# Second feed-forward product: 8 of 22 row tiles in seven-product form, and modulation matmuls offered later

## The chip, the cores and the metric

The kernel runs on one core of a Trainium2 chip. The metric is the device time of one execution in microseconds. Five engines run side by side and wait for one another through semaphores: TensorE (PE: matmul, with its weight loads shown apart as PEld), VectorE (DVE), ScalarE (ACT), GpSimd (POOL), and SyncE (SP), which here issues all DMAs, in one order. Matmul results land in PSUM, which has eight banks of 512 fp32 columns in this kernel's use.

## The reference

Two layers of a hybrid decoder. One prompt of 512 positions and 8 sampled sequences of one position each go through the same weights, so a tile of activations has 520 columns. Cut to what matters here:

```python
mod = jax.nn.silu(c) @ ada_w + ada_b          # 1024 -> 6 x 1024 for each of 9 conditions
sh_m, sc_m, gt_m, sh_f, sc_f, gt_f = split(mod, 6)
h = rmsnorm(x, g_pre_mix) * (1 + sc_m) + sh_m
proj = h @ w_in                               # 1024 -> 2816, then retention, two convolutions
mix = concat([o_ret, o_a, o_c]) @ w_out       # 1024 -> 1024
x = x + gt_m * rmsnorm(mix, g_post_mix)
h = rmsnorm(x, g_pre_ffn) * (1 + sc_f) + sh_f
f = (jax.nn.silu(h @ ffn_w1) * (h @ ffn_w3)) @ ffn_w2   # 1024 -> 2816 -> 1024
x = x + gt_f * rmsnorm(f, g_post_ffn)
```

All is fp32.

## The kernel before

**Layout.** Activations stand feature by position: a feature tile is 128 partitions x 520 columns, worked on in two halves of 260 (h = 0 and 1; half 1 holds the sampled columns). An fp32 product is made from parts: each operand is split into a high part (a cast to fp32r, by ACT) and a low part (operand minus high, by DVE or POOL), and `mm3` (L721) issues three matmuls, high x high, high x low and low x high, into one PSUM bank. Weights come in units of 128 x 1024 (512 KB), eight 128 x 128 blocks: a DMA fills one of 3 "raw" buffers, ACT casts it ("wh"), DVE subtracts ("wl"). The split units live in a ring of 8 "w" slots, two to a unit; `ensure_unit` (L682), `ensure_raw` (L654) and `unit` (L1403) claim them in the order of a list of specs. Larger temporaries live in a ring of 22 "s" slots, two big ones ("hh") hold H, the normalized input, and Y, the output.

**Order.** The order of every engine's instructions is fixed when the program is built, by a planner: `Clock` holds estimated times, `Eng` estimates the cost of each operation, background jobs are generators that yield the time at which they want to go on (`at`, L128: the estimated time at which a tile is ready, moved by `lead`), and `mm` moves the planner's time on. `either` (L267) gives an operation to DVE or POOL, whichever the planner expects to end first. On the chip each engine then takes its instructions in that order and waits on semaphores where the estimate was off.

**Modulation.** `ada` (L356) computes a third of the modulation: four times it starts four DMAs of 512 KB of `ada_w`, yields until they are estimated to have landed (L367), and then offers a burst of 16 matmuls (`fill`), which is placed where the planner sees PE waiting, or at the latest a gap after the yield's start (4.5 us in layer 0's input projection, 9 in layer 1's, 12 in layer 0's first feed-forward product). The next four DMAs follow the burst. Two groups of four bursts run beside the input projection of each layer (L1739); `ck.join(ada_bg)` (L1743) has the planner wait for them ahead of the output projection. One more group, for layer 1, runs beside the first feed-forward product.

**First feed-forward product.** 22 row tiles of 128 of the hidden width. Tiles 0 and 1 are plain. Tiles 2 to 21 use a seven-product form (Strassen, Winograd's variant): the 2 x 2 blocks are w1 and w3 by two halves of the depth, against the two halves of the depth by two halves of the columns. `zprep` (L743) makes seven split weight products ("wz", each 128 x 512, one w slot) named A11, S1, S2, A12, S3, A22 and S4; `Operands` makes the sums T1 to T4 of H; `zproduct` (L838) does 4 x 3 matmuls for a product. Sums of products are formed in PSUM, by going on in a bank or a copy of it. The gated result stays in `FT` (pairs of row tiles, fp32) and `fparts` splits it into `F` (high, low).

**Second feed-forward product** (L2009 to L2040). For each output tile m of 8 and half h, 22 row tiles are summed in one bank: 66 matmuls. Tile 0 does both halves side by side, in the order in which `F` becomes ready. A weight unit serves both halves; in layer 0 half 1 of tile 5 comes last, with its three units read again; the first two units of tile 6 stand in an hh buffer ("wq"). ACT copies each bank to Y and squares it for the norm. When half 0 has its eight tiles, a `Chain` (L569) applies the norm and the gate, adds to x and, in layer 0, makes H for layer 1's input projection, while PE does what is left of half 1.

## Time and profile before

| | |
|---|---|
| time, median of 3 runs | 1208.46 us (1208.44 to 1209.1) |
| the profiled execution's own time | 1211.95 us |
| its span, first to last instruction | 1210.1 us |
| mean granted TensorE clock | 0.993 |
| bytes moved by DMA | 175.52 MB, 145 GB/s on average |
| second product of layer 0 | 489.13 to 616.62 us |
| second product of layer 1 | 1071.86 to 1198.60 us |

The page gives busy times of engines, the chain of work that ended last, and groups of instructions by cost. Nearly all DVE, ACT and POOL instructions have the line of one helper (L176) and nearly all matmuls that of `mm` (L243), so groups are told apart by tile names: "ps<-s,wz" is a matmul into PSUM with a wz weight and an operand in an s slot, "s,sc" a modulation matmul, "t,one" the matmul that sums squares over partitions. In the stretches view each engine's busy time is followed by its count of instructions; the three figures at the end are the granted clock, the DMA engines' share and GB/s. In the order of time a row has start, duration, engine, and in brackets the idle time before it and what ended it; PE's instructions overlap, so starts are compared, not durations.

### The profile page before, as it was taken

How to read it: one execution, taken by the hardware profiler on the slowest of the kernel's cores; microseconds unless marked ns; L12 is line 12 of the kernel's file. 1: busy time of each engine (PE TensorE's matmuls, PEld its weight loads, DVE VectorE, ACT ScalarE, POOL GpSimd, SP SyncE). 2: the span in 40 equal slices, each digit the busy share in tenths (PEclk: the TensorE clock that was granted, in tenths of full speed). 3: DMA queues.
4: the chain of work that ended last, by engine and by line, in shares of the span. 5: the costliest groups of instructions: out<-in, count | busy, mean ns of one | idle time of the engine just before them, and what ended most of it. 6: DMA issues, size and time to landing. Idle time of an engine off the chain costs nothing.

```text
span 1210.1 us, 24224 instructions
## 1 busy us (share of the span) xinstructions
PE 1187.4 (98%) x9795; PEld 1124.7 (93%) x9795; DVE 885.5 (73%) x1608; ACT 624.8 (52%) x1254; POOL 155.6 (13%) x155
## 2 busy tenths in 40 slices
PE   9999999999999999999999999999999999999996
PEld 8878779999989999999988879899999999999996
DVE  6679868689979988623493489878999998882234
ACT  6553454577546556623352354466765555582221
POOL 0284102011100000000004334200110000010001
PEclk9999999999999999999999999899999999999998
DMA  8578674424673232333365854343323343142222
GB/s 310 223 193 254 237 261 83 145 87 143 214 254 123 89 124 81 114 96 101 113 250 215 266 169 144 71 141 104 123 73 109 135 140 114 61 127 81 83 77 72
DMA packets 71073, 175.52 MB, mean 145 GB/s; under 512 B 23857, under 2 KB 28593, under 8 KB 70961
## 3 DMA queue, kind: packets, MB, share of 16 engines
q1 hardware_dynamic: 70960, 173.97, 44.0%
q8 instruction: 77, 1.26, 0.4%
q14 instruction: 36, 0.29, 0.1%
HBM read 166.74 MB, written 5.08 MB: 142 GB/s over the span
## 4 chain that ended last, share of the span: by engine, by line
PE 80%; DVE 9%; ACT 3%; DMA 3%; POOL 2%; issue 2%; SPq 1%; POOLq 0%; DVEq 0%; ACTq 0%
PE ps L243 80%; DVE s L176 3%; DVE t L176 2%; DMA s<-in_ada_w_dram 2%; POOL s L176 2%; DVE wl L176 1%; DVE ps L176 1%; DVE H L176 1%; ACT s L176 1%; SPq L258 1%; PE ps L253 1%; ACT wh L176 1%; ACT t L176 1%; ACT L176 1%; ACT H L176 0%
## 5 line engine op out<-in xcount | busy, mean ns | idle before, releaser
L243 PE MATMUL ps<-s,wh 128*128 128x260 f32 x1536 | 277.5, 283 | 0.0
L243 PE MATMUL ps<-s,wz 128*128 128x260 f32 x1920 | 246.3, 283 | 0.3 <-ACT ps L176 0.2
L243 PEld LDWEIGHTS ps<-s,wz 128*128 128x128 f32 x1920 | 236.6, 188 | 3.7 <-issue 2.5
L243 PEld LDWEIGHTS ps<-s,wh 128*128 128x128 f32 x1536 | 236.9, 188 | 0.3
L243 PE MATMUL ps<-H,wh 128*128 128x260 f32 x1184 | 228.7, 292 | 1.4 <-ACT s L176 1.0
L243 PE MATMUL ps<-s,wl 128*128 128x260 f32 x768 | 216.8, 282 | 0.0
L243 PEld LDWEIGHTS ps<-H,wh 128*128 128x128 f32 x1184 | 185.5, 191 | 20.0 <-issue 15.1
L176 DVE TENSOR_TENSOR wl<-raw,wh 128x1024 fp32r<-128x1024 f32 (+1 forms) x92 | 115.3, 1259 | 78.3 <-ACT wh L176 77.8
L243 PE MATMUL ps<-H,wl 128*128 128x260 f32 x592 | 168.4, 284 | 0.3 <-DVE wl L176 0.3
L243 PE MATMUL ps<-H,wz 128*128 128x260 f32 x1104 | 147.8, 283 | 0.0
L243 PEld LDWEIGHTS ps<-s,wl 128*128 128x128 f32 x768 | 144.5, 188 | 0.0
L243 PEld LDWEIGHTS ps<-H,wz 128*128 128x128 f32 x1104 | 138.5, 188 | 1.2 <-issue 0.8
L176 ACT CAST wh<-raw 128x1024 fp32r<-128x1024 f32 (+1 forms) x95 | 94.9, 1009 | 38.3 <-PE ps L243 27.8
L176 ACT CAST wz<-raw 128x512 fp32r<-128x512 f32 x144 | 87.7, 620 | 51.3 <-DVE raw L176 39.8
L243 PEld LDWEIGHTS ps<-H,wl 128*128 128x128 f32 x592 | 113.0, 191 | 0.6 <-DVE wl L176 0.6
L176 DVE TENSOR_TENSOR wz<-raw,wz 128x512 fp32r<-128x512 f32 x144 | 97.8, 687 | 16.9 <-ACT wz L176 14.9
L243 PE MATMUL ps<-H,s 128*128 128x260 f32 (+1 forms) x816 | 106.1, 285 | 1.3 <-ACT s L176 1.3
L243 PEld LDWEIGHTS ps<-H,s 128*128 128x128 f32 x816 | 100.9, 188 | 4.4 <-issue 2.1
L176 DVE TENSOR_TENSOR t<-t,t 128x260 f32<-128x260 f32 x99 | 42.1, 431 | 80.0 <-ACT t L176 78.1
L176 DVE TENSOR_TENSOR wz<-s,wz 128x512 fp32r<-128x512 f32 x108 | 73.7, 686 | 16.6 <-ACT wz L176 15.9
L176 ACT COPY s<-ps 128x260 f32<-128x260 f32 (+1 forms) x83 | 35.4, 434 | 92.1 <-PE ps L243 70.0
L243 PE MATMUL ps<-s,s 128*128 128x260 f32 (+3 forms) x672 | 79.3, 287 | 0.0
(166 smaller groups left out, 1585.0 us busy)
## 6 DMA issues: line engine op xcount, KB each, us to landing
raw<-in_w_dram SPq DMA_DIRECT2D x102, 512.0 KB, 3.6
s<-in_ada_w_dram SPq DMA_DIRECT2D x80, 512.0 KB, 6.3
raw<-in_w_in_dram SPq DMA_DIRECT2D x38, 512.0 KB, 4.5
s<-in_w_dram SPq DMA_DIRECT2D x34, 512.0 KB, 5.2
raw<-in_w_dram SPq DMA_DIRECT2D x25, 384.0 KB, 4.2
s<-in_ada_dram SPq DMA_DIRECT2D x16, 512.0 KB, 7.5
raw<-in_w_out_dram SPq DMA_DIRECT2D x16, 512.0 KB, 4.6
X<-in_xT_dram SPq DMA_DIRECT2D x4, 520.0 KB, 5.5
```

Of the source, the lines that this page charges most:

```text
L176: f(*args, **kw)
L243: PE.matmul(out, lhsT, rhs, start=start, stop=stop, skip_group_check=True)
L253: PE.transpose(out, in_, ident[:n, :n])
L258: nc.sync.dma_start(out=out, in_=in_)
```

## The change

**Second feed-forward product.** Its 22 row tiles are taken in three pieces, with the running sum kept in Y between them. First row tiles 16 to 21, plain, for all eight output tiles (tiles 0 and 1 side by side, row tiles 16 to 19 ahead of 20 and 21); the banks are copied to Y. Then row tiles 8 to 15 in the seven-product form: the 2 x 2 blocks are two output tiles by two groups of four row tiles, against the two groups by the two halves of the columns, four pairs of output tiles. A job `names` makes the split operands B11, B22, B21 and T1 to T4 from `FT[3]` to `FT[6]`, in part in an hh buffer (`ext`); `zprep` makes the weight products with the w2 blocks (tag "zz") as its raw data; `plus` adds the results into Y. Last row tiles 0 to 7, plain, first half 0 of all output tiles, then half 1 (tile 7 first): `back` has ACT copy Y into a bank two jobs ahead, the matmuls go on summing there, and the result is copied to Y as before. The weights of this piece are read once for each half, except for tile 7; the rereading of tile 5 in layer 0 and the buffer "wq" go.

**Split of the gated rows.** `fparts` takes a list of pairs: pairs 7 and 8 (row tiles 16 to 19) at the end of the first product, pairs 0 to 2 (2 to 7) during the seven products. Pairs 3 to 6 are no longer split themselves.

**Modulation.** The job yields until 3 us after the estimated landing of its weights in place of the landing itself; with a gap that is over by then, the burst is placed at once. This holds for all five groups.

**Weight supply.** `ensure_unit` returns where no slot or raw buffer is free, and `unit` lets the planner's time go on until there is one.

```diff
--- before.py
+++ after.py
@@ -364,7 +364,7 @@
                 dma(r, ada_w[l, k1 * 128:(k1 + 1) * 128, c0:c0 + 1024], ck.now)
                 ts.append(r)
             t0 = ck.now
-            yield at(*ts)
+            yield ck.at(*ts, lead=-3.0)
             if ps is None:
                 ps = bank()
...
             if rawlive["raw"] == 3:
-                if tag != "z" or rawlive["s"] >= 2:
+                if tag[0] != "z" or rawlive["s"] >= (2 if tag == "z" or zspare[0] else 1):
                     return
...
-    def zprep(l, t):
+    def zprep(l, t, pairs=()):
...
+        for p in pairs:
+            order += [(p, "A11"), (p, "S1")] + [(p - 1, "A22"), (p - 1, "S4")] * (p > pairs[0])
+            order += [(p, "S2"), (p, "A12"), (p, "S3")]
+        if pairs:
+            order += [(pairs[-1], "A22"), (pairs[-1], "S4")]
...
+                if pairs:
+                    j1, j3 = U["w2", l, 2 * (i - pairs[0]), 1], U["w2", l, 2 * (i - pairs[0]) + 1, 1]
...
-        for j in ([U["w1", l, NZ], U["w3", l, NZ]] if NZ < NF else [U["w2", l, 0, 0], U["w2", l, 0, 1]]):
+        for j in [U["w2", l, 0, 0], U["w2", l, 1, 0]] if pairs else [U["w2", l, 0, 2], U["w2", l, 1, 2]]:
...
         for m in range(KT):
-            for u in range(3):
-                n = min(8, NF - 8 * u)
-                U["w2", l, m, u] = spec(w2[l, m, :, u * 1024:u * 1024 + n * 128], n=n,
-                                        tag=f"q{u}" if m == 6 and u < 2 else "w")
-        if l < DEPTH - 1:
-            for u in range(3):
-                n = min(8, NF - 8 * u)
-                U["w2", l, KT, u] = spec(w2[l, MR, :, u * 1024:u * 1024 + n * 128], n=n)
+            U["w2", l, m, 2] = spec(w2[l, m, :, 2048:2048 + 768], n=6)
+        for m in range(KT):
+            U["w2", l, m, 1] = spec(w2[l, m, :, 1024:2048], tag="zz")
+        for m in range(KT):
+            U["w2", l, m, 0] = spec(w2[l, m, :, 0:1024])
+        for m in range(KT - HOLD):
+            U["w2", l, m, 3] = spec(w2[l, m, :, 0:1024])
 
...
     def unit(key, ahead=2):
         i = U[key]
         ensure_unit(i)
+        while i not in units:
+            ck.wait()
+            ensure_unit(i)
...
-        def fparts():
-            n = len(FT)
-            for j in range(n):
-                while j >= allow[0]:
+
+        def fparts(js):
+            for n, j in enumerate(js):
+                while n >= allow[0]:
                     yield 0.05
-                src = FT[j] if j < n - 1 else fx[0]
+                src = FT[j]
                 p = slot(F32R), slot(F32R)
...
-                ck.start(fparts())
+                allow[0] = ALLOW[0]
+                ck.start(fparts([7, 8]))
...
-        jobs = [(m, h) for m in range(6) for h in range(2)] + [(6, 0), (7, 0), (7, 1), (6, 1)]
-        if not last:
-            jobs.remove((MR, 1))
...
+        def names():
+
+            def src(q, h):
+                return [FT[3 + 2 * q + n][:, :, cols(h)] for n in range(2)]
+
+            def put(name, x, home=None):
+                for n in range(2):
+                    t = slot(F32R, (128, 2, 2, HW)) if home is None else ext[:, home + 2 * n:home + 2 * n + 2]
+                    yield at(x[n])
+                    S.copy(out=t[:, :, 0, :], in_=x[n])
+                    yield at(t[:, :, 0, :])
+                    yield from turn(-1)
+                    V.tensor_tensor(out=t[:, :, 1, :], in0=x[n], in1=t[:, :, 0, :], op=sub)
+                    nt.setdefault(name, []).append(t)
+
+            def tsum(x, y, z):
+                for n in range(2):
+                    yield from turn(-1)
+                    V.tensor_tensor(out=x[n], in0=y[n], in1=z[n], op=sub)
+
+            b11, b12, b21, b22 = src(0, 0), src(0, 1), src(1, 0), src(1, 1)
+            yield from put("B11", b11)
+            yield from tsum(b11, b12, b11)
+            yield from put("T1", b11, 0)
+            yield from put("B22", b22)
+            yield from tsum(b12, b22, b12)
+            yield from tsum(b22, b22, b11)
+            yield from put("T2", b22, 4)
+            yield from put("B21", b21)
+            yield from tsum(b21, b21, b22)
+            while not zspare[0]:
+                yield 0.05
+            yield from put("T3", b12)
+            yield from put("T4", b21)
+
+        zspare[0] = False
+        ck.start(names(), 6.0)
+        P0 = NF + 1
+        ck.start(zprep(l, ck.now, list(range(P0, P0 + 4))))
...
+        acc = [(m, h, bank()) for m in range(2) for h in range(2)]
+        for ks in (range(16, 20), range(20, NF)):
+            for m in range(2):
+                un = unit(("w2", l, m, 2), 1)
+                for k in ks:
+                    while k not in F:
+                        ck.wait()
+                    for m1, h, ps in acc:
+                        if m1 == m:
+                            whole2(m, 2, h, k, un, ps, k == 16, k == NF - 1)
+        for m, h, ps in acc:
+            S.copy(out=Y[:, h, m, :], in_=ps[:, :HW])
+        for m in range(2):
+            free_unit(("w2", l, m, 2))
+        for m in range(2, KT):
+            un = unit(("w2", l, m, 2), W2A)
+            for h in range(2):
+                ps = bank()
+                for k in range(16, NF):
+                    whole2(m, 2, h, k, un, ps, k == 16, k == NF - 1)
+                S.copy(out=Y[:, h, m, :], in_=ps[:, :HW])
+            free_unit(("w2", l, m, 2))
+        for k in range(16, NF):
+            del F[k]
+        zspare[0] = True
+        allow[0] = 3
+        mp, ybg = {}, {}
+        def zq(p, b, ps, name, first, copied=None):
+            while len(nt.get(name, ())) < 2:
+                ck.wait()
+            zproduct(l, P0 + p, b, ps,
+                     lambda k: (nt[name][k // 2][:, k % 2, 0, :], nt[name][k // 2][:, k % 2, 1, :]), first, copied)
+        def plus(h, m, x):
+            def job():
+                yield atp(x) if in_psum(x) else at(x)
+                either(Y[:, h, m, :], x, Y[:, h, m, :], add)
+            ybg.setdefault((h, m), []).append(ck.start(job()))
+        def m_first(p):
+            a, d = bank(), bank()
+            zq(p, "A11", a, "B11", True)
+            b = bank()
+            S.copy(out=b[:, :HW], in_=a[:, :HW])
+            zq(p, "S1", d, "T1", True)
+            mp[p] = [a, d, b]
+        def m_up(p):
+            a, x3 = mp[p][0], mp[p][3]
+            zq(p, "A22", a, "T4", False, x3)
+            plus(0, 2 * p + 1, a[:, :HW])
+        def m_gate(p):
+            d = mp.pop(p)[1]
+            zq(p, "S4", d, "B22", False)
+            plus(1, 2 * p, d[:, :HW])
+        for p in range(4):
+            m_first(p)
+            if p == 0:
+                ck.start(fparts([0, 1, 2]))
+            else:
+                m_up(p - 1)
+                m_gate(p - 1)
+            a, d, b = mp[p]
+            zq(p, "S2", a, "T2", False)
+            x2 = tmp()
+            S.copy(out=x2, in_=a[:, :HW])
+            plus(1, 2 * p, x2)
+            zq(p, "A12", b, "B21", False, b[:, :HW])
+            plus(0, 2 * p, b[:, :HW])
+            zq(p, "S3", a, "T3", False, x2)
+            x3 = tmp()
+            S.copy(out=x3, in_=a[:, :HW])
+            plus(1, 2 * p + 1, d[:, :HW])
+            plus(1, 2 * p + 1, x3)
+            mp[p].append(x3)
+        jobs = [(m, 0) for m in range(KT)]
+        jobs += [(m, 1) for m in range(KT - HOLD, KT)] + [(m, 1) for m in range(KT - HOLD)]
...
+        def back(n):
+            m, h = jobs[n]
+            for x in ybg[h, m]:
+                ck.join(x)
+            ps = bank()
+            S.copy(out=ps[:, :HW], in_=Y[:, h, m, :])
+            pre.append(ps)
+        back(0)
+        back(1)
+        for n, (m, h) in enumerate(jobs):
+            ps = pre[n]
+            if n == 1:
+                m_up(3)
+            if n == KT:
+                m_gate(3)
+            if n + 2 < len(jobs):
+                back(n + 2)
+            key = ("w2", l, m, 3 if h and m < KT - HOLD else 0)
+            while key not in units and U[key] not in units and wlive[0] > 6:
+                ck.wait()
+            un = unit(key, W2A)
+            ck.to(max(ck.now, ck.ready(ps[:, :HW])))
+            for k in range(8):
...
+                whole2(m, 0, h, k, un, ps, False, k == 7)
+            if h == 1 or m < KT - HOLD:
+                free_unit(key)
+            if not last and h == 1:
+                ensure_unit(U["in", l + 1, KGRP], U[key])
```

## The prediction

> **What bounds the kernel now.** I read the page from the top: span, busy time, chain that ended last.

> ```profile
> span 1210.1 us, 24224 instructions
> ...
> PE 1187.4 (98%) x9795; PEld 1124.7 (93%) x9795; DVE 885.5 (73%) x1608; ACT 624.8 (52%) x1254; POOL 155.6 (13%) x155
> ...
> PE 80%; DVE 9%; ACT 3%; DMA 3%; POOL 2%; issue 2%; SPq 1%; POOLq 0%; DVEq 0%; ACTq 0%
> ```

> TensorE (PE) is busy 98% and is 80% of the chain: fewer matmuls is time, provided that what feeds them keeps up. Whether it does is read by stage, in the stretches view (PE, weight load, DVE, ACT, sometimes POOL, then clock, DMA share, GB/s).

> ```profile
> 361.00:421.00 60.00, 60.00 (x503) 59.18 (x495) 52.44 (x98) 35.78 (x78) 0.00 (x0) 1.00 0.34 114
> ...
> 489.13:616.62 127.49, 127.49 (x1063) 127.30 (x1062) 56.11 (x87) 50.52 (x86) 1.63 (x2) 1.00 0.33 102
> ...
> 593.00:617.00 24.00, 24.00 (x199) 23.81 (x198) 20.47 (x42) 13.66 (x25) 1.63 (x2) 1.00 0.32 106
> 617.00:640.00 23.00, 22.05 (x175) 19.67 (x174) 21.68 (x43) 13.12 (x28) 4.42 (x5) 1.00 0.87 328
> ```

> The first row lies in the first feed-forward product, which already has the seven-product form: DVE is busy 52.44 of 60 us (87%) and PE still never idles. The second is the whole second product of layer 0 (489.13 is its first matmul, 616.62 the first of layer 1): there DVE has 71 us free. The last two are the passage into layer 1, where DVE is busy 20.47 of 24 and 21.68 of 23: nearly the bound, and PE begins to lose time.

> The other losses of PE are waits. The order of time shows the modulation matmuls ("s,sc") that wait for their weights, and what one burst of 16 costs undisturbed (640.90 to 642.76):

> ```profile
> 82.26 1.65 PE L243 MATMUL ps<-s,sc 128*32 128x512 f32 x8
> 85.08 1.05 PE L243 MATMUL ps<-s,sc 128*32 128x512 f32 x4 [1.17 <-DMA s<-in_ada_w_dram]
> 87.45 1.75 PE L243 MATMUL ps<-s,sc 128*32 128x512 f32 x4 [1.32 <-DMA s<-in_ada_w_dram]
> 89.12 0.80 PE L243 MATMUL ps<-H,wh 128*128 128x260 f32 x2
> ...
> 91.18 0.40 PE L243 MATMUL ps<-H,wh 128*128 128x260 f32 x2
> ```
> ```profile
> 640.90 1.92 PE L243 MATMUL ps<-s,sc 128*32 128x512 f32 x16
> 642.76 0.51 PE L243 MATMUL ps<-H,s 128*128 128x260 f32 x2
> ```
> ```profile
> 677.14 1.96 PE L243 MATMUL ps<-s,sc 128*32 128x512 f32 x12
> 679.77 1.05 PE L243 MATMUL ps<-s,sc 128*32 128x512 f32 x4 [0.67 <-DMA s<-in_ada_w_dram]
> 680.75 0.50 PE L243 MATMUL ps<-H,wh 128*128 128x260 f32 x2
> ```

> **Part one: the seven-product form.** Before, each layer does 8 output tiles x 22 row tiles x 2 halves x 3 matmuls = 1056. After: 6 row tiles plain (288), 8 row tiles as 4 pairs x 7 products x 4 x 3 = 336 in place of 384, and 8 row tiles plain (384): 1008. So 48 go per layer, 96 in all. Their price is the pace of the same form in the first product:

> ```profile
> 447.14 3.05 PE L243 MATMUL ps<-s,wz 128*128 128x260 f32 x24
> ...
> 457.22 3.05 PE L243 MATMUL ps<-s,wz 128*128 128x260 f32 x24
> ```

> The lines between hold 60 matmuls, so 84 starts take 10.08 us, 0.120 us each. 96 x 0.120 = **11.5 us removed**. It is on the path: PE is busy throughout the stage.

> It adds vector work. Prices, by group in the order-by-cost view of 361 to 421 us, and by the order of time at 480 us:

> ```profile
> L176 DVE TENSOR_TENSOR wz<-raw,wz 128x512 fp32r<-128x512 f32 x24 | 16.2, 686 | 2.3 <-ACT wz L176 1.9
> ...
> L176 DVE TENSOR_TENSOR t<-ps,t 128x260 f32<-128x260 f32 x14 | 5.9, 423 | 0.0
> L176 DVE TENSOR_TENSOR raw<-raw,raw 128x512 f32<-128x512 f32 x7 | 4.8, 687 | 0.1
> ```
> ```profile
> 479.11 1.92 DVE L176 TENSOR_TENSOR s<-s,s 128x520 fp32r<-128x520 f32 x3
> ...
> 481.28 0.69 DVE L176 TENSOR_TENSOR s<-s,s 128x520 fp32r<-128x520 f32 x1
> 481.89 1.22 DVE L176 TENSOR_TENSOR wl<-raw,wh 128x1024 fp32r<-128x1024 f32 x1
> ...
> 485.95 1.25 DVE L176 TENSOR_TENSOR s<-s,s 128x520 fp32r<-128x520 f32 x1
> ```

> Per layer: 28 low parts of weight products x 0.686 = 19.2; 16 sums of weight blocks x 0.687 = 11.0; 14 low parts and 8 differences of the operands x 0.69 = 15.2; 24 additions into Y x 0.42 = 10.1; less 8 plain units x 1.22 = 9.8. That is +45.7. The weights of the last eight rows are read twice for seven of eight tiles, where layer 0 now rereads one tile (3 units): +4 x 1.22 = 4.9. So 56.1 + 45.7 + 4.9 = 107 us of DVE in 1008 x 0.120 = 121 us, 88%. The first product runs at 87% with no PE idle, and by the line of three (1.92 us) neighbours overlap, so 107 is on the high side. Cover exists for the stage as a whole.

> Not for each piece of it. The seven-product piece is 336 x 0.120 = 40.3 us. Its DVE work is 4 x (7 x 0.686 + 4 x 0.687 + 6 x 0.42) = 40.3, plus T3 and T4 (4 x 0.69) and three splits of pairs for later rows (6 x 0.69): 47.2 us. The eight w slots allow about six units ahead (6 x 0.686, and 3 sums: 6.2), which leaves 41.0. Between the ends, 0 and 47.2 - 40.3 = 6.9 us per layer (below 0 is excluded: PE has no idle there to win), I take 0.75 per layer, near the row of 87% with PE idle at nothing: **+1.5**. Queued behind a product whose unit is late are all later matmuls on PE, and behind those the ACT copies of the sums and the next pair's additions.

> The first six row tiles are now needed at once, tiles 20 and 21 after 48 matmuls (5.8 us); today the split of the last one ends at about 490.4, 1.3 us after the stage begins:

> ```profile
> 489.98 0.42 DVE L176 TENSOR_TENSOR s<-t,s 128x260 fp32r<-128x260 f32 x1
> ```

> So nothing; should that cover go, at most the last gate's length. ACT gains 14 operand casts, 16 copies of Y back into PSUM and the like, but is busy 50.52 of 127.49: nothing, with the passage below as its tight place. Weights in the last 46 us come at 512 KB per 24 matmuls (2.9 us), 182 GB/s; the stretch 617 to 640 moves 328: nothing, with SP's queue behind it if a raw buffer is late.

> **The passage into layer 1.** Half 0 now ends 8 jobs x 24 x 0.120 = 23.0 us before the stage does; today 3 x 66 x 0.120 = 23.8. In those 23 us DVE gets 1 to 4 more weight splits (1.2 to 4.9) and five more sums of squares (5 x 0.42 = 2.1), 3.3 to 7.0 against 24 - 20.47 = 3.5 free, and 0.8 less cover. So H of half 0 is late by 0.6 to 4.3. I take **+2**, layer 0 alone; behind it wait the first projections of layer 1. Some sums can go to POOL, and PE is short of 23.00 - 22.05 = 0.95 in the last stretch already: the ends are -0.95 and 4.3.

> But POOL is no free helper: the 0.69 us operation took 1.25 at 485.95, and beside it ran

> ```profile
> 485.26 1.38 POOL L176 TENSOR_TENSOR t<-t,t 128x260 f32<-128x260 f32 x1 [0.93 <-ACT t L176]
> ```

> That costs DVE 0.56, more than the 0.42 of an addition handed over. [...]

> **Part two: modulation matmuls.** They are offered 3 us after the estimated landing. The wait at 82.26: the burst took 89.12 - 82.26 = 6.86 against 1.86 undisturbed. Started 3 us later, at 85.26, its last four come at 85.26 + 12/16 x 1.92 = 86.70, and their tile lands at 87.45: 0.75 remains. Gain 6.86 - 1.86 - 0.75 = 4.25. After it PE ran at half clock:

> ```profile
> 87.70:91.00 3.30, 3.30 (x12) 1.88 (x9) 0.17 (x1) 1.04 (x1) 0.43 (x2) 0.50 0.84 110
> ```

> From 89.12 to 91.18 there are 9 matmuls, 2.06 for 1.08: 1.0 more. The second, 680.75 - 677.14 = 3.61, loses 1.75. Sum 7.0. The ends are 7.7 (without the 0.75) and -1.9 (one burst more in PE's way, below). I take **5.5**, since what PE then meets is not all PE's doing: SP brings the rope pieces and these weights in one order,

> ```profile
> 74.26 2.50 SPq L258 DMA_DIRECT2D s<-s  x4
> 76.80 2.03 SPq L258 DMA_DIRECT2D s<-in_ada_w_dram  x4
> 78.94 0.65 SPq L258 DMA_DIRECT2D raw<-in_w_in_dram  x1
> ```

> and an earlier PE may wait for those instead. The next burst's four DMAs are issued after the burst, so they too come up to 3 us later on SP, and projection weights pass ahead of them: no harm. Eight bursts x 3 = 24 us more for layer 0's series; its last is now at 178.18, and the output projection ("s,wh"), ahead of which the program waits for the series, starts at 205.63. Those 27 us are just enough; if not, that last burst (1.92) stands in front of it with no projection work left to hide its landing.

> ```profile
> 178.18 1.92 PE L243 MATMUL ps<-s,sc 128*32 128x512 f32 x16
> ...
> 205.63 0.41 PE L243 MATMUL ps<-s,wh 128*128 128x260 f32 x2
> ```

> **Sum:** -11.5 + 1.5 + 2.0 - 5.5 = -13.5. The profiled execution took 1211.95 (span 1210.1); the median of the three shown is 1208.46. I take the difference to the median: **1195.0 us**.

> **The rivals.** (a) *The modulation wait only moves*: 1195.0 + 5.5 = 1200.5. For it: the rope rows above. Against it: DVE itself stood idle for want of PE, and would start earlier too:

> ```profile
> 90.83 0.43 DVE L176 TENSOR_TENSOR s<-ps,t 128x260 f32<-128x260 f32 x1 [4.36 <-PE ps L243]
> ```

> [...]

> (b) *Better*: no new wait, and the order of layer 1 comes out without

> ```profile
> 774.59 1.23 PE L243 MATMUL ps<-t,one 128*128 128x260 f32 x2 [2.78 <-DVE t L176]
> ```
> ```profile
> 724.00:775.00 51.00, 48.22 (x378) 45.26 (x377) 49.33 (x79) 21.76 (x37) 21.25 (x13) 0.99 0.36 109
> ```
> ```profile
> 773.80:780.50 6.70, 5.91 (x25) 5.72 (x26) 2.88 (x6) 0.73 (x2) 0.00 (x0) 0.50 0.63 142
> ```

> 2.78 plus half of 6.7 at half clock = 6.1. 1208.5 - 11.5 - 5.5 - 6.1 = 1185.4. Against it: DVE is busy 49.33 of the 51 us before, so the wait is DVE's work, which the change leaves.

> (c) *Slower: DVE sets the pace of the second product.* 2 x 6.9 = 13.8, and the passage at 4.3 with half of 6.7 at half clock, 3.4: 21.5. 1208.5 - 17.0 + 21.5 = 1213.0. It decides once new waits pass 17.0 + 2.4 = 19.4 us. For it: 47.2 us of work in 40.3, in order on one queue. Against it: the 87% row.

> (d) *No change*: (c) at four fifths, about 1208.

> (e) *It does not do what it says*: where a burst waits for its gap anyway (12 us in the first product), 3 us alter nothing; neither wait above lies there, so this has no chance of its own.

> **How the numbers follow.** Forecast 0.45 (own range 1190 to 1199); (a) 0.20; (b) 0.15; (c) 0.09; (d) 0.11, of it 0.06 within 0.2% (about 2.4 us, what a measurement here can tell from no change). Faster 0.45 + 0.20 + 0.15 + 0.05 = 0.85, same 0.06, slower 0.09. Range 1184 to 1206: forecast, (a), most of (b) and a little of (d), 0.8.

> **What would show it.** Right: 96 fewer matmuls; the stage from the last "wz" of the first product to layer 1's first matmul near 121 to 125 us; PE busy throughout the stretch of seven products; no "in_ada_w_dram" wait over 1 us; one half-clock window gone. Wrong: in the waits view, PE waiting for DVE "wz" or ACT "ps" inside the second product, or for DVE "H" at layer 1's start by over 4 us; a new PE wait for rope pieces near 95 us; the wait at 771 grown.

## The result, and the profile after

| | before | after |
|---|---|---|
| median of 4 runs each, same chip | 1208.78 us (1208.44 to 1209.43) | **1194.78 us** (1194.41 to 1195.92) |
| ratio, 95% interval | | 0.9884 (0.9870 to 0.9897) |
| the profiled execution: time, span | 1211.95, 1210.1 us | 1195.92, 1193.7 us |

The change saves 14.0 us; the prediction said 13.5 and 1195.0 us. That the sum is right does not make its terms right, so they are taken one by one below. First the page of the changed kernel: span, busy time of each engine, and the chain that ended last.

```profile
span 1193.7 us, 24444 instructions
...
PE 1173.1 (98%) x9699; PEld 1111.1 (93%) x9699; DVE 969.3 (81%) x1763; ACT 680.7 (57%) x1403; POOL 159.0 (13%) x159
...
PE 31%; DVE 3%; ACT 1%; issue 0%
```

PE has 96 matmuls fewer (9795 to 9699), and PE, DVE and ACT have moved towards one another: DVE from 73% to 81%. The chain's shares add up to 35%: it could be followed back only so far, and says nothing of what lies ahead of that.

The stretches view of the changed kernel (columns as before): the second product of layer 0, its run of seven-product matmuls, and the two sides of layer 1's first matmul at 609.90.

```profile
486.04:609.90 123.86, 122.60 (x1015) 121.92 (x1013) 98.52 (x164) 80.72 (x164) 9.30 (x7) 1.00 0.40 127
520.60:558.15 37.55, 37.55 (x313) 37.37 (x312) 34.63 (x62) 23.35 (x46) 4.31 (x2) 1.00 0.34 112
585.60:609.90 24.30, 23.79 (x197) 23.49 (x195) 23.04 (x43) 18.65 (x40) 5.00 (x5) 1.00 0.51 161
609.90:633.00 23.10, 21.55 (x171) 19.09 (x170) 22.34 (x43) 13.85 (x29) 5.79 (x6) 1.00 0.78 292
```

The seven-product run shows PE busy 37.55 of 37.55 us beside a DVE at 92%. (It holds 26 of the 28 products; of the last two, one comes behind the first plain tile, at 562.18, and the other just ahead of half 1, at 583.88.)

To see where the time went, the span is cut at starts of matmuls that every version has. The lengths in us, worked out from the order of time:

| up to | before | after | later offer alone | seven products alone | after, offer moved in layer 0 only | after, in layer 1 only |
|---|---|---|---|---|---|---|
| layer 0's output projection, first matmul | 205.63 | 202.75 | 200.24 | 202.49 | 200.13 | 202.85 |
| its second product | 283.50 | 283.28 | 283.86 | 283.26 | 283.28 | 283.30 |
| layer 1's first matmul | 127.48 | 123.86 | 127.45 | 123.67 | 123.84 | 123.68 |
| layer 1's output projection | 180.38 | 175.35 | 177.02 | 179.51 | 179.58 | 175.38 |
| its first seven-product matmul | 92.59 | 92.59 | 92.73 | 96.94 | 95.35 | 92.53 |
| its second product | 182.27 | 182.16 | 182.49 | 182.22 | 182.20 | 181.63 |
| the last matmul of that | 126.63 | 122.33 | 126.81 | 122.62 | 122.19 | 122.36 |
| the end | 11.61 | 11.37 | 11.47 | 11.29 | 11.32 | 11.30 |

The two second products give 3.6 + 4.3 = 7.9 us, layer 1's input projection 5.0 and layer 0's 2.9. (The spans differ by 16.4 us and the medians by 14.0: the profiled execution of the kernel before stood 3.2 above its median, that of the changed kernel 1.1. So a stage of the first column can be longer than in a median execution by up to some 3 us.) The last four columns belong to the experiments.

### The profile page after: what moved, and what is told of

The parts are those of the page before. It is cut to its first block, busy times and chain, and to the rows that moved or that the text cites. A ratio compares the mean times of both kernels' runs of the same rounds, so it can differ in the third digit from the quotient of the medians.

```text
span 1193.7 us, 24444 instructions
## 1 busy us (share of the span) xinstructions
PE 1173.1 (98%) x9699; PEld 1111.1 (93%) x9699; DVE 969.3 (81%) x1763; ACT 680.7 (57%) x1403; POOL 159.0 (13%) x159
## 3 DMA queue, kind: packets, MB, share of 16 engines
q8 instruction: 76, 1.25, 0.4%
## 5 line engine op out<-in xcount | busy, mean ns | idle before, releaser
L243 PE MATMUL ps<-s,wz 128*128 128x260 f32 x2400 | 307.4, 283 | 0.4 <-ACT ps L176 0.4
L243 PEld LDWEIGHTS ps<-s,wz 128*128 128x128 f32 x2400 | 295.5, 188 | 3.8 <-issue 2.5
L243 PE MATMUL ps<-H,wh 128*128 128x260 f32 x1184 | 226.3, 290 | 0.4 <-DVE H L176 0.4
L243 PE MATMUL ps<-s,wh 128*128 128x260 f32 x1152 | 209.0, 283 | 1.5 <-ACT ps L176 1.5
L243 PEld LDWEIGHTS ps<-H,wh 128*128 128x128 f32 x1184 | 182.8, 188 | 19.0 <-issue 14.9
L243 PEld LDWEIGHTS ps<-s,wh 128*128 128x128 f32 x1152 | 177.9, 188 | 2.2 <-ACT ps L176 1.9
L243 PE MATMUL ps<-H,wz 128*128 128x260 f32 x1296 | 173.3, 283 | 0.0
L243 PE MATMUL ps<-H,wl 128*128 128x260 f32 x592 | 167.1, 282 | 0.5 <-DVE wl L176 0.5
L243 PEld LDWEIGHTS ps<-H,wz 128*128 128x128 f32 x1296 | 162.8, 188 | 1.2 <-issue 0.8
L243 PE MATMUL ps<-s,wl 128*128 128x260 f32 x576 | 162.8, 283 | 0.0
L176 DVE TENSOR_TENSOR wl<-raw,wh 128x1024 fp32r<-128x1024 f32 (+1 forms) x92 | 113.3, 1237 | 55.6 <-ACT wh L176 54.2
L176 ACT CAST wz<-raw 128x512 fp32r<-128x512 f32 x178 | 108.4, 620 | 64.2 <-DVE raw L176 52.2
L176 DVE TENSOR_TENSOR wz<-raw,wz 128x512 fp32r<-128x512 f32 x178 | 121.4, 690 | 20.3 <-ACT wz L176 18.5
L243 PEld LDWEIGHTS ps<-H,wl 128*128 128x128 f32 x592 | 111.5, 188 | 0.9 <-DVE wl L176 0.9
L243 PEld LDWEIGHTS ps<-s,wl 128*128 128x128 f32 x576 | 108.4, 188 | 0.0
L176 DVE TENSOR_TENSOR wz<-s,wz 128x512 fp32r<-128x512 f32 x130 | 88.7, 686 | 22.5 <-ACT wz L176 21.8
L243 PE MATMUL ps<-H,s 128*128 128x260 f32 (+1 forms) x816 | 105.5, 284 | 1.3 <-ACT s L176 1.3
L243 PEld LDWEIGHTS ps<-H,s 128*128 128x128 f32 x816 | 100.8, 188 | 3.6 <-ACT s L176 2.0
L176 ACT CAST wh<-raw 128x1024 fp32r<-128x1024 f32 (+1 forms) x94 | 94.5, 1014 | 3.3 <-DMA raw<-in_w_in_dram 2.1
L176 ACT CAST wz<-s 128x512 fp32r<-128x512 f32 x130 | 79.5, 619 | 26.6 <-DVE s L176 18.9
L176 DVE TENSOR_TENSOR s<-s,s 128x520 fp32r<-128x520 f32 (+4 forms) x114 | 82.6, 746 | 7.1 <-ACT s L176 6.4
L176 ACT COPY s<-ps 128x260 f32<-128x260 f32 (+1 forms) x83 | 35.4, 434 | 90.5 <-PE ps L243 69.3
```

The source lines that it names most:

```text
L176: f(*args, **kw)
L243: PE.matmul(out, lhsT, rhs, start=start, stop=stop, skip_group_check=True)
```

## The experiments

**Each part alone.** In the kernel before, the first line; in the changed kernel, the second:

```diff
-            yield at(*ts)
+            yield ck.at(*ts, lead=-3.0)
```
```diff
-            yield ck.at(*ts, lead=-3.0)
+            yield at(*ts)
```

> The kernel before with the modulation matmuls offered 3 us later, and nothing else. The prediction's term: -5.5 us against the kernel before, 1203.3. The stages of the two profiles (layer 0 up to the second product -3.1, layer 1 up to the second product -5.1): -8.2, 1200.6. If the profiled run of before was a slow one of its kind (1211.95 against a median of 1208.8) and the seven-product form alone gives -7.9, what is left of the measured -14.0 is -6.1: 1202.7. Rival (the wait only moves): no change, 1208.8. In its profile: the first burst of layer 0 near 2.5 us instead of 7.1, and the wait of 2.8 us near 771 either still there (then the seven-product form took it away) or gone (then the later offer did).

> The changed kernel with the modulation matmuls offered at the estimated landing again. The prediction's terms: -11.5 + 3.5 = -8.0 against the kernel before, 1200.8. The stages of the profiles (second product -3.6 in layer 0, -4.3 in layer 1): -7.9, the same. If the two parts help each other (the wait near 771 needs both), less: 1204. The first burst of layer 0 should again take 7 us with half clock behind it.

The later offer alone: 1203.81 us (1203.35 to 1204.08), ratio 0.9951 (0.9937 to 0.9966), 5.7 us saved where 5.5 was predicted. The seven products alone: 1204.12 us (1202.45 to 1206.45), ratio 0.9958 (0.9943 to 0.9973): 5.4 saved where 8.0 was predicted. A miss, and an instructive one: by the table the two second products give the same 3.8 and 4.0 us as in the full change. What is lacking is lost in layer 1: its input projection keeps its long wait, and the stage behind it, from the output projection to the first seven-product matmul, is 4.35 us longer than before. PE's order of time in this kernel:

```profile
771.61 1.23 PE L243 MATMUL ps<-t,one 128*128 128x260 f32 x2 [3.38 <-DVE t L176]
...
788.60 0.68 PE L243 MATMUL ps<-t,one 128*128 128x260 f32 x2 [1.38 <-DVE t L176]
...
796.27 0.51 PE L243 MATMUL ps<-s,wh 128*128 128x260 f32 x2 [1.24 <-ACT wh L176]
...
797.53 0.39 PE L243 MATMUL ps<-s,wl 128*128 128x260 f32 x1 [0.75 <-DVE wl L176]
```

The wait that stood at 774.59 before (2.78 us) has grown to 3.38, and behind the last two the clock went to half (as behind the first, from 771.30 to 774.70), by the stretches view:

```profile
798.60:802.00 3.40, 3.40 (x18) 3.40 (x17) 1.24 (x2) 1.65 (x5) 0.00 (x0) 0.50 0.91 286
```

1.24 + 0.75 + half of 3.4 are 3.7 of these 4.35 us. So the two parts meet at this place, and the seven products without the later offer make it worse.

**Is the second product bound by PE or by DVE?** One kernel leaves out three quarters of product S4 of each pair (72 matmuls in all, 72 x 0.120 = 8.6 us); the other adds 32 additions of 128 x 260 per layer to DVE's queue inside the seven-product piece, which nothing reads.

```diff
-        for k in range(4):
+        for k in range(1 if short else 4):      # short for "S4"
```
```diff
+            for _ in range(8):
+                V.tensor_tensor(out=tmp(), in0=X[:, 0, cols(0)], in1=X[:, 1, cols(0)], op=add)
```

> The changed kernel with three quarters of the product S4 of each pair left out (9 of 12 matmuls, 72 in all); all work of DVE and ACT stays. If PE sets the pace of the seven-product piece: -72 x 0.120 = -8.6 us against the changed kernel, 1186.1. If DVE sets the pace: no change, 1194.8. DVE is idle 2.9 us of that piece, so where PE saves 4.3 per layer, DVE becomes the bound after 2.9: -5.8 to -8.6 is what PE-bound with little to spare would give.

> The changed kernel with eight more DVE additions of 128x260 (0.34 us from start to start) for each pair of output tiles in the seven-product piece, 32 per layer, 10.9 us of DVE; nothing reads them. In that piece DVE is busy 34.6 of 37.6 us. If DVE has only those 2.9 us to give, PE loses 10.9 - 2.9 = 8 per layer: +16 against the changed kernel, 1211. If the work ahead (weight products, additions into Y) can slide into the pieces beside, less: +4 to +10. If DVE were no near bound at all: 0.

Fewer matmuls: 1187.65 us (1187.14 to 1188.07), ratio 0.9818 (0.9802 to 0.9834). The stages of the second products shrink by 3.96 and 3.10 of 4.32 each: 82% of what is taken from PE comes out as time. More vector work: 1213.19 us (1212.88 to 1214.23), ratio 1.0035 (1.0023 to 1.0048). The two stages grow by 9.1 and 9.5. The additions last 0.42 us each, but neighbours overlap: two of this shape in a row take 0.76 us at 528.42 in the changed kernel, 0.34 from start to start. By that the 64 of them, in eights, occupy DVE for 22.4 us, 11.2 per layer. PE's waits in layer 0 there, in order of time:

```profile
536.20 4.45 PE L243 MATMUL ps<-s,wz 128*128 128x260 f32 x34 [1.13 <-DVE wz L176]
544.90 0.80 PE L243 MATMUL ps<-H,wz 128*128 128x260 f32 x2 [4.25 <-ACT wz L176]
546.34 2.54 PE L243 MATMUL ps<-H,wz 128*128 128x260 f32 x10 [0.64 <-DVE wz L176]
```

The longest wait names ACT, but ACT itself waited, by its own order of time:

```profile
543.19 0.62 ACT L176 CAST wz<-raw 128x512 fp32r<-128x512 f32 x1 [3.56 <-DVE raw L176]
```

It stood for a sum of weight blocks from DVE. And PE's clock was at half beside it, in the stretches view:

```profile
543.10:549.90 6.80, 4.36 (x18) 4.06 (x19) 6.66 (x12) 3.70 (x7) 0.00 (x0) 0.50 0.48 154
```

1.13 + 4.25 + 0.64 and half of 6.8 make 9.4, the 9.1 of the stage. So the changed kernel stands between two edges: taking from PE pays nearly in full, and 11 us more for DVE, in a run where it is idle for 2.9, costs nine. (They stand eight in a row, so their place may count beside their amount.) This is the prediction's rival (c), brought about by added work; it shows that the mechanism exists and how far away it was.

**The joint of the pieces.** What the change loses in the second product lies for the most part not in the seven-product run but right behind it. PE's order of time in the changed kernel:

```profile
557.30 1.13 PE L243 MATMUL ps<-s,wz 128*128 128x260 f32 x8
559.18 0.51 PE L243 MATMUL ps<-s,wh 128*128 128x260 f32 x2 [0.75 <-ACT ps L176]
```

From the last seven-product start (558.15) to the first plain one (559.18) pass 1.03 us instead of 0.12; at 1131.96 in layer 1 the same. ACT's order of time beside it:

```profile
558.47 0.38 ACT L176 COPY t<-ps 128x260 f32<-128x260 f32 x1 [1.56 <-PE ps L243]
558.74 1.00 ACT L176 COPY ps<-Y 128x260 f32<-128x260 f32 x3
```

The copies of Y into PSUM (ps<-Y), for which the plain matmuls wait, need nothing of the last product; but ahead of them in ACT's order stands the copy out of that product's bank (t<-ps). ACT idles 1.56 us for PE, then PE idles 0.75 for ACT. The experiment issues the first two copies one product earlier:

```diff
+            if p == 3:
+                back(0)
+                back(1)
             # ahead of product "S3" of the last pair
...
-        back(0)
-        back(1)
```

> The changed kernel with the first two copies of Y back into PSUM issued on ACT ahead of the copy of the last product of the seven, instead of behind it. Theory (PE waits 0.91 us at the joint of the pieces in each layer because ACT takes these copies in order behind one that needs the last product): -1.8 us against the changed kernel, 1193.0, and the gap at the joint falls from 1.03 to about 0.12 us. Rival (the weight unit or the additions into Y are late there as well): the gap stays above 0.5, time within 0.5 us of the changed kernel.

1191.24 us (1191.20 to 1192.65), ratio 0.9851 (0.9835 to 0.9867). The stages shrink by 1.05 and 1.03 us. PE's order of time in it:

```profile
554.67 3.05 PE L243 MATMUL ps<-s,wz 128*128 128x260 f32 x24
557.55 0.40 PE L243 MATMUL ps<-s,wh 128*128 128x260 f32 x2
```

24 starts x 0.120 = 2.88 = 557.55 - 554.67: no gap is left. The stages account for 2.1 us; the medians of different rounds differed by 3.5. A second pair of runs, side by side on one chip:

> The copies alone once more, beside the changed kernel on the same chip. Theory: 3 to 4 us below the changed kernel if both earlier medians hold, of which the two joints give 2.1 and the rest is layer 0's first stage, which differs from run to run by a microsecond or two. Rival: the joints give 2.1 and nothing else: 1192.7 against 1194.8.

> The changed kernel itself, as the measure for the two runs beside it. Theory: 1194.8 us, half a microsecond either way, and no half clock between 760 and 800 us. Rival: the wait in layer 1 (1.40 us) is near enough to the point where the clock falls that it falls in some executions: then the runs spread by 3 us or more, as those of the kernel before do.

1191.16 us (1191.02 to 1191.39), ratio 0.9852 (0.9831 to 0.9873), beside 1193.94 us (1192.93 to 1194.51), ratio 0.9874 (0.9856 to 0.9892). That is 2.8 us between them: 2.0 in the two second products, the rest mostly in layer 0's input projection, which neither version touches. The changed kernel itself had 202.75 us there in one profile and 201.20 in the other; so differences under about 2 us in that stage mean nothing. Half clock between 760 and 800 us appeared in neither. This version beats both kernels.

**Where does the later offer pay?** It is kept for one layer's input projection at a time, by the gap (4.5 in layer 0, 9 in layer 1; the fifth group, with 12, keeps the early offer in both); and doubled for all.

```diff
-            yield ck.at(*ts, lead=-3.0)
+            yield ck.at(*ts, lead=-3.0 if gap == 4.5 else 0.0)   # layer 0 only; 9.0: layer 1 only
```
```diff
+            yield ck.at(*ts, lead=-6.0)                          # twice as late, for all
```

> The changed kernel with the modulation matmuls offered 3 us later in layer 0's input projection alone. Theory (in layer 1 the later bursts let the convolution's chain on DVE end sooner against PE, which is what removed the wait near 771 and its half clock): that wait is back at 2.8 us or more with half clock behind it, the stage from layer 1's first matmul to its output projection is 179 to 180 us instead of 175.4, time +4 to +5 against the changed kernel, 1199. Rival (the seven-product form, or the earlier arrival from layer 0, removed it): 1195.

> The changed kernel with the modulation matmuls offered 3 us later in layer 1's input projection alone. The first burst of layer 0 takes 5 to 7 us again (2.5 with the later offer), the seventh 2.06 again (4.2 with it: its weights landed late). The prediction's term: +5.3 against the changed kernel, 1200. By what two runs without the later offer show (205.63 and 202.49 us to the output projection against 202.75): 0 to +3, and a wider spread from run to run, since half clock follows the wait in some runs only.

> The changed kernel with 6 us in place of 3. The prediction: a series of eight bursts stretched by 24 us fits the 27 us ahead of the output projection just enough; by 48 us it doesn't. Layer 0's last burst then stands in front of the output projection: +2 to +15 against the changed kernel, 1197 to 1210, in the stage up to the output projection of layer 0. Layer 1 has 60 us to spare and should not lose. If the planner's wait costs PE nothing on the chip: same, 1195.

| kept for | us | ratio, 95% interval |
|---|---|---|
| layer 0 only | 1200.28 (1199.67 to 1202.29) | 0.9931 (0.9918 to 0.9944) |
| layer 1 only | 1194.95 (1194.69 to 1195.73) | 0.9884 (0.9869 to 0.9899) |
| all, 6 us late | 1207.20 (1205.45 to 1210.08) | 0.9983 (0.9972 to 0.9994) |

Moved in layer 1 only, the whole gain is there; moved in layer 0 only, 5.3 us of that are lacking, on the same chip. PE's order of time shows the wait of layer 1, with layer 0 moved only:

```profile
769.37 1.07 PE L243 MATMUL ps<-t,one 128*128 128x260 f32 x2 [3.38 <-DVE t L176]
```

with layer 1 moved only:

```profile
760.33 0.68 PE L243 MATMUL ps<-t,one 128*128 128x260 f32 x2 [1.10 <-DVE t L176]
```

and in the changed kernel:

```profile
760.35 0.68 PE L243 MATMUL ps<-t,one 128*128 128x260 f32 x2 [1.12 <-DVE t L176]
```

What ends it is a square "t" on DVE, behind the convolutions. DVE's order of time before, and after:

```profile
767.99 0.74 DVE L176 SCALAR_TENSOR_TENSOR ps<-s,par,ps 128x512 f32<-128x512 f32 x1
...
769.17 1.67 DVE L176 TENSOR_SCALAR s<-s,par 128x512 f32<-128x512 f32 x1
...
774.12 0.42 DVE L176 TENSOR_TENSOR t<-s 128x260 f32<-128x260 f32 x1
```
```profile
753.23 1.54 DVE L176 SCALAR_TENSOR_TENSOR ps<-s,par,ps 128x512 f32<-128x512 f32 x2
...
759.78 0.42 DVE L176 TENSOR_TENSOR t<-s 128x260 f32<-128x260 f32 x1
...
760.96 1.23 DVE L176 TENSOR_SCALAR s<-s,par 128x512 f32<-128x512 f32 x1
```

The first row of each is the last of the convolutions' 48 steps. Before, it starts 767.99 - 616.62 = 151.4 us after the layer's first matmul; after, the second of the two at 754.0, 144.1 after it. The square follows about 6 us later in both. Over the versions the chain's last step comes at 144 where layer 1's bursts are offered later (after, layer 1 only, later offer alone), at 151 before, and at 158 with seven products and no later offer in layer 1 (two versions). The bursts themselves do not wait in layer 1 in any version with seven products: each takes 1.9 to 2.3 us there. So what the later offer changes in layer 1 is where the convolutions stand in DVE's order: 14 us, where nothing else differs (144 with layer 1 moved only, 158 with the seven products alone). Counted from the program's end, 659 of DVE's instructions are left from that last step on in the former, 645 in the latter.

The rows show what this order does to PE. A group of six operations, about 3 us long, begins with the TENSOR_SCALAR "s<-s,par". Before, at 769.17, it stands ahead of the square that PE waits for; after, at 760.96, behind it. All thirteen traces fit: the group stands ahead of the awaited square in the four with a wait of 2.78 us or more there (before, seven products alone, layer 0 moved only, all 6 us late), and behind it in the nine with 1.42 or less. Why the planner orders it so was not tried.

In layer 0 the offer did what was meant, and it was worth little: 0.2 us by the medians (1194.95 to 1194.78, from different rounds), some 1.5 by the profiles (below). The burst at 82.26 us with its two waits of 1.17 and 1.32 is now this, in PE's order of time, with the seventh burst of the series:

```profile
84.98 2.41 PE L243 MATMUL ps<-s,sc 128*32 128x512 f32 x16
```
```profile
183.88 1.62 PE L243 MATMUL ps<-s,sc 128*32 128x512 f32 x8
185.68 1.05 PE L243 MATMUL ps<-s,sc 128*32 128x512 f32 x4 [0.17 <-DMA s<-in_ada_w_dram]
186.93 1.05 PE L243 MATMUL ps<-s,sc 128*32 128x512 f32 x4 [0.20 <-DMA s<-in_ada_w_dram]
```

From the matmul ahead of a burst to the one behind it, the first takes 2.55 us against 5.21 with the early offer in layer 0, the seventh 4.24 against 2.06: 2.66 won, 2.18 given back. The series has slid into a time in which its weights are slow to land. The transfers view at 168 to 190 us:

```profile
s<-in_ada_w_dram SPq DMA_DIRECT2D x8, 512.0 KB, 11.4
```

A median of 11.4 us from issue to landing; before, the burst at that place (issued in 160 to 176 us) had

```profile
s<-in_ada_w_dram SPq DMA_DIRECT2D x4, 512.0 KB, 7.6
```

With 6 us the slide goes over the edge. The last bursts of the series stand directly ahead of the output projection, by PE's order of time:

```profile
195.72 1.05 PE L243 MATMUL ps<-s,sc 128*32 128x512 f32 x4 [0.86 <-DMA s<-in_ada_w_dram]
197.16 1.05 PE L243 MATMUL ps<-s,sc 128*32 128x512 f32 x4 [0.39 <-DMA s<-in_ada_w_dram]
198.44 1.05 PE L243 MATMUL ps<-s,sc 128*32 128x512 f32 x4 [0.23 <-DMA s<-in_ada_w_dram]
199.71 0.62 PE L243 MATMUL ps<-s,sc 128*32 128x512 f32 x2 [0.22 <-DMA s<-in_ada_w_dram]
```

The stage up to layer 0's output projection takes 208.16 us, 5.4 more than in the changed kernel, and layer 1's takes 182.08, 6.7 more. The latter was not expected. The long wait is back, by PE's order of time:

```profile
777.86 1.24 PE L243 MATMUL ps<-t,one 128*128 128x260 f32 x2 [4.37 <-DVE t L176]
```

The convolutions end early here, 139 us after the layer's first matmul, but the group of six stands ahead of the awaited square (772.28 against 777.39). So a later offer is not better by itself: what counts is the order that comes of it.

**The early copies, and in layer 0 the first burst alone later.** If the first burst gains and the seventh gives back, moving only the first should keep the gain.

```diff
-            yield ck.at(*ts, lead=-3.0)
+            yield ck.at(*ts, lead=-3.0 if gap == 9.0 or k == 0 and g == 1 else 0.0)
```

> The copies of the last four blocks ahead of the last S3 product, and the later offer for all of layer 1's bursts but in layer 0 for the first burst alone (the seventh then keeps its early offer, as it had when only layer 1 was moved: 2.06 us). Theory: the two gains add: the joint gives 1.0 per layer, and layer 0's stage up to the output projection falls from 202.8 to about 200.6 (first burst 2.5 and seventh 2.06 at once): 1189 us. Rival: that stage is set by the projection matmuls around the bursts and by the rope waits, not by the bursts, so what a burst loses less is lost at another wait: then the time is that of the copies alone, 1191.

1192.10 us (1191.58 to 1193.18), ratio 0.9861 (0.9843 to 0.9879), beside 1191.16 with the copies alone: no gain. The first and the seventh burst both take 2.06 us now, but the second has a wait instead, by PE's order of time:

```profile
102.02 2.05 PE L243 MATMUL ps<-s,sc 128*32 128x512 f32 x12
104.29 1.05 PE L243 MATMUL ps<-s,sc 128*32 128x512 f32 x4 [0.22 <-DMA s<-in_ada_w_dram]
```

It takes 3.45 us: its transfers are issued behind the first burst, which is 3 us later, while the burst itself is offered at the landing again. The rival holds: a wait taken away at one burst of this series comes back at another.

## Why the prediction was right, point by point

- **96 matmuls, -11.5: right.** The count is 9699, the second products are PE's, and 82% of a further cut came out as time. The 7.9 us that the two stages give are these 11.5, less 3.2 of longer gaps between single starts (1.8 of them at the joints), less 0.4 because the other starts lie 0.0002 us further apart.
- **Pacing in the seven-product piece, +1.5: the size is right, the reason is wrong.** DVE does not pace it: PE idles nowhere in 520.60 to 558.15. The step that failed is "47.2 ... which leaves 41.0" us of work in 40.3. DVE's groups add up to 39.2 us of busy time in that run (26 products, 37.55 us), but together they occupy only 34.63, since neighbours overlap; the prediction had noted this for the stage as a whole and not for the piece. The loss stands at the joint: 2 x (1.03 - 0.12) = 1.8 us, in ACT's order, which the prediction had at nothing ("ACT gains 14 operand casts, 16 copies of Y back into PSUM and the like, but is busy 50.52 of 127.49: nothing"). The sign of being wrong that it named, a wait of PE for ACT "ps" inside the second product, did show: 0.75 us at each joint. Early copies win that back.
- **The first six row tiles, 0, and the transfers of the last piece, 0: right.** No wait of PE for either shows.
- **The passage into layer 1, +2: right in kind, about half in size.** PE's idle time there, from the stretches, is 0.51 + 1.55 us against 0 + 0.95 before: +1.1. DVE is at 23.04 of 24.30, so it is the bound named. PE's order of time has the waits:

```profile
603.28 0.68 PE L243 MATMUL ps<-t,one 128*128 128x260 f32 x2 [0.51 <-DVE t L176]
611.49 0.39 PE L243 MATMUL ps<-H,wl 128*128 128x260 f32 x1 [0.48 <-DVE wl L176]
613.95 0.71 PE L243 MATMUL ps<-t,one 128*128 128x260 f32 x2 [0.30 <-DVE t L176]
619.89 0.39 PE L243 MATMUL ps<-H,wh 128*128 128x260 f32 x1 [0.43 <-DVE H L176]
```

- **DVE beside POOL: it cost little.** The planner gave POOL only two operations in the seven-product run (4.31 us), and DVE did not pace PE. DVE's low parts in it, by the order-by-cost view,

```profile
L176 DVE TENSOR_TENSOR wz<-raw,wz 128x512 fp32r<-128x512 f32 x14 | 10.0, 724 | 0.0
```

  take 724 ns on average against 686 in the first product, where POOL was idle: 14 x 0.038 = 0.5 us. All of it is one operation, which starts at 536.48 beside POOL's addition of 535.88 to 537.17 and takes 1.24 us; the other thirteen take 0.68 to 0.69. Beside POOL's other addition, of 526.09 to 529.12, none of DVE's operations of 0.69 us is longer. So a loss like the 0.56 us that the prediction read at 485.95 came with one of the two additions, and PE, busy throughout, does not feel it.
- **The later offer, -5.5: the total is right (5.7 alone), the place is wrong beside the seven products.** The prediction took it from two bursts that wait, 5.25 at 82.26 and 1.75 at 677.14. For the first, the bursts that change are the first and the seventh of the series. Together they take 7.1 and 7.3 us in the two seven-product versions with the early offer in layer 0, and 5.0 to 6.8, on average 5.7, in the eight traces with it 3 us later: 1.5 won. The stage's lengths agree (202.5 and 202.9 against 201.2 on average), but they spread by 2.6. Part of the 5.25 was that one execution: with the same early offer the first burst took 5.1 and 5.2 us in those two versions, against 7.1 before, with no half clock behind it. The second wait is gone in every version with seven products, the offer moved or not. What pays beside the seven products is the wait near 771, which rival (b) priced and the prediction took for "DVE's work, which the change leaves". DVE's work stayed; its order did not. From the start before to the start after it lost 3.06 to 1.40 us, 1.66 won, and the 6.7 us at half clock behind it, 3.35 won: 5.0, which is the stage's 180.38 - 175.35. This is one execution of each, and that of the kernel before had a granted clock of 0.993, where most of its runs had 0.995 to 0.997. The figure from medians is the 5.3 between the two single layers.
- **What was right by luck.** The terms do not add: 5.7 alone and 5.4 alone make 11.1, together they give 14.0. They are coupled through layer 1's wait, which the seven products alone make longer and the later offer makes shorter. Counted on top of the later offer, the seven products give 0.9951 to 0.9884, or 8.1 us, the 8.0 of the prediction.
- **Open:** in layer 0 the offer seems to win 3.8 us when layer 1's is not moved (1204.12 to 1200.28, from different rounds) and nothing when it is (1194.95 to 1194.78). Of the former, 1.8 of the 4.1 us between the two profiles lie in stages after layer 0's (96.94 to 95.35 among them), where one has a second half-clock stretch and the other not; it was not settled. Nor was how the 5.7 of the offer alone divide: between its profile and that of the kernel before, layer 0's stage is 5.4 us shorter and layer 1's 3.4, but the latter profile stood 3.2 above its median.

## What to carry to other kernels

A fixed order on an engine couples places far apart: before a small shift of one kind of work is priced at the wait it is aimed at, look which chains of another engine it reorders, and test each place alone, since two wrong terms can make a right sum. Where a piece of work hands over to the next through a copy, put the copy ahead of the last result that it does not need. And add occupied time, not durations, when an engine's work in a stretch is held against the stretch.

## What the hardware showed that was not expected

**The clock.** A single wait of PE of 1.1 to 1.4 us was followed by no half clock (1.12 after, 1.42 with the later offer alone, at the same place). Waits of 2.78, 3.38 (in two versions) and 4.25 us were, each time. With layer 0 moved only, the stretches view has right behind the wait:

```profile
769.60:773.00 3.40, 3.40 (x15) 3.21 (x15) 1.33 (x5) 1.66 (x3) 0.00 (x0) 0.50 0.45 159
```

```profile
795.19:798.60 3.41, 1.58 (x10) 1.37 (x11) 2.35 (x2) 3.41 (x7) 0.00 (x0) 1.00 0.06 11
793.50:796.91 3.41, 1.97 (x14) 1.77 (x15) 2.68 (x3) 3.41 (x7) 0.00 (x0) 1.00 0.11 28
```

PE is idle for 1.83 us of the first piece and for 1.44 of the second; half clock follows the first only. In the kernel before, the pieces ahead of the two half-clock stretches, 84.25 to 87.67 and 770.29 to 773.70, have PE idle for 2.15 and 1.89 us, and no other piece at full clock up to the last matmul for more than 0.70. In the changed kernel the most is 1.12 (757.81 to 761.23), and the clock stays full up to the last matmul. What follows on 1.44 to 1.83 us is not shown. A wait of about 3 us thus costs 5 to 6 here (3.38 and half of 3.4, 2.78 and half of 6.8), and one of 1.12, as in the changed kernel, costs itself alone. The kernel before, which has such a long wait, spread over 1206.1 to 1212.6 us in its 41 runs; the changed kernel over 1192.9 to 1195.9 in eight. That the waits fall on the pieces differently from run to run would explain it, but it was not shown: only one of the 41 has a trace.
